# Decoder block on one core: the first loads reordered, in smaller pieces of weights, with one of them issued by ScalarE and nine warming products in place of twelve

## The chip, the cores and the metric

The kernel runs on one core of a Trainium2 chip. The core has TensorE (PE in the profile, with PEld for its weight loads), VectorE (DVE), ScalarE (ACT), GpSimd (POOL) and SyncE (SP), which here only issues transfers. The metric is the time of one execution in device microseconds (us), as the median of a few runs.

## The reference, cut to what matters

One decoder block on 512 tokens of 1024 features: a norm, one wide projection whose parts feed a stick-breaking attention and a recurrence, then a gated merge, an MLP and a gated embedding. The change lies in the first lines only: the norm and the first columns of the projection.

```python
def rms_norm(x, g):
    y = xf * lax.rsqrt(jnp.mean(xf * xf, axis=-1, keepdims=True) + NORM_EPS)
    return y * g
...
h = rms_norm(x, attn_norm_g[i])
u = h @ w_in[i]                       # 1024 x 5376 columns, all of them needed
u_sb, u_rw, u_gate = jnp.split(u, [SB_COLS, SB_COLS + RW_COLS], axis=-1)
q, k, v = jnp.split(u_sb.reshape(bsz, seq, 3 * SB_HEADS, SB_HEAD_DIM), 3, axis=2)
o_sb = stick_breaking_attention(q, k, v)
```

## The kernel before, in words

Activations lie with features on the 128 partitions and tokens along the free axis, so x is eight tiles of 128x512 (`x_in`, one for each k of 0 to 7). The norm is split in two. Each tile of x is multiplied by its gain, a column of the small table `cols`, and goes into the products at once. The factor 1/rms of a token (`rs`) is applied behind the products, when `ps_m` or `ps_z` is read.

Every matrix product is made from three products of rounded parts. A value is split in a high part (ScalarE rounds it: `w_hi`, `h_hi`) and a rest (VectorE subtracts: `w_lo`, `h_lo`). `mm3` issues high by high (L191), rest of x by high weights (L192) and high x by rest of weights (L193). So a tile k of x needs ScalarE (L353) and VectorE (L354) once before any product with it, and each unit of weights needs the same (L221 and L222 in the first two units, L175 and L176 in the later ones).

A unit of weights is 128x1024: eight blocks of 128x128, one for each k. `seq` lists the units in order of use. The first units are q (unit 0), k (unit 1) and v (unit 2) of the first pair of heads, then q, k and v of the second pair (units 3, 4 and 5). For units 0 and 1 the products of both are taken turn by turn for each tile of x, so 6 products for each k, 48 in all. Then come the 24 products of unit 2, then those of unit 3, and so on. The raw weights of a unit go to one of two buffers (`w_raw`), so that the load of unit n waits until the split of unit n-2 is done.

Ahead of the first real product TensorE multiplies a tile of zeros (`warm`) several times.

While the first units are loaded and multiplied, ScalarE squares the tiles of x (L227 for k = 0, L230 for the others, two buffers `sq`), and VectorE sums the squares (`ssum`, L232 and L234). One product (L263) then sums over the partitions; ScalarE and VectorE make `rs` from it (L253 to L257). With `rs`, VectorE reads the first three results (`qT` L394, `kT` L406, `vT` L414), ScalarE and GpSimd round q (`qq`), ScalarE and VectorE split k (`kk`, L409 and L410). TensorE transposes v (L421) and starts the scores (L458).

The instructions are not issued in the order of the code. A scheduler of the framework puts those of each engine into one fixed order when the kernel is built, by its own estimates of when each is ready; a DMA stands in the order of the engine that issues it. At run time each engine takes its instructions in that order and stops at one whose inputs are late. An early difference in the code can so move instructions further on. Each DMA has one of eight semaphores in turn, so an issue waits for the landing of the DMA eight before it.

Of the kernel before, what the change touches and what calls it, by code (L numbers as in the profile page):

```python
# [18 lines left out]
P = 128  # L19
# [66 lines left out]
def tile_block(ctx: ExitStack, tc: tile.TileContext, xT, xt, pT, wts, lora, cols_d, gfin_d, consts_d, out, dbg=None):  # L86
    nc = tc.nc
    act, dve, pool, pe, sync = nc.scalar, nc.vector, nc.gpsimd, nc.tensor, nc.sync
# [3 lines left out]
    def r32(ap):  # L92
        return ap.bitcast(F32)
# [12 lines left out]
    cols = const.tile([P, NCOLS], F32, name="cols")  # L106
# [12 lines left out]
    def col(name, i):  # L119
        return cols[:, COLS[name] + i:COLS[name] + i + 1]  # L120
# [32 lines left out]
    def unit(i):  # L153
        return wts[UBASE[seq[i][0]] + seq[i][1]]
# [65 lines left out]
    def split(hi, lo, src):  # L220
        act.copy(out=hi, in_=src)  # L221
        dve.tensor_tensor(out=lo, in0=src, in1=r32(hi), op=ALU.subtract)  # L222
# [54 lines left out]
    with ExitStack() as sA:  # L277
# [43 lines left out]
        with ExitStack() as s1:  # L321
# [3 lines left out]
            def ps_z():  # L325
                return ps1.tile([P, T], F32, name="ps_z", bufs=5)
# [5 lines left out]
            warm = p1.tile([P, T], BF16, name="warm", tag="sp")  # L332
            pool.memset(warm, 0.0)
            ps = ps_z()
            for _ in range(12):
                pe.matmul(ps, warm[:, 0:P], warm, start=True, stop=True)
            sync.dma_start(out=cols, in_=cols_d)
            ssum = p1.tile([P, T], F32, name="ssum", tag="wl")

            raws = [wpool.tile([P, 1024], F32, name="w_raw", bufs=2) for _ in range(2)]  # L340
            first_w = [[wpool.tile([P, 1024], F32R, name=n) for n in ("w_hi", "w_lo")] for _ in range(2)]
            xs_in = {}

            def first_weights(i, part):
                cs = slice(part * 512, part * 512 + 512)
                sync.dma_start(out=raws[i][:, cs], in_=unit(i)[:, cs])
                split(first_w[i][0][:, cs], first_w[i][1][:, cs], raws[i][:, cs])

            def first_x(k):
                x_in = p1.tile([P, 2, T], F32, name="x_in", tag=("sp", "sph", "spl", "wh")[k // 2]) if k % 2 == 0 else xs_in[k - 1][0]  # L350
                sync.dma_start(out=x_in[:, k % 2, :], in_=xT[:, k, :])
                xs_in[k] = x_in, x_in[:, k % 2, :]
                act.activation(out=h_hi[:, k, :], in_=xs_in[k][1], func=AF.Copy, scale=col("attn_g", k))  # L353
                dve.scalar_tensor_tensor(out=h_lo[:, k, :], in0=xs_in[k][1], scalar=col("attn_g", k), in1=r32(h_hi[:, k, :]),  # L354
                                         op0=ALU.mult, op1=ALU.subtract)


            first_weights(0, 0)
            first_x(0)
            first_weights(1, 0)  # L360
            for k in range(1, 4):
                first_x(k)
            first_weights(0, 1)
            first_weights(1, 1)
            for k in range(4, KT):
                first_x(k)
            loaded.extend(raws)
# [892 lines left out]
    def gated(ps, tt, cs, i, own=False, behind=None):  # L1260

        n = ps.shape[-1]
        t = p4.tile([P, T], F32, name="t4", bufs=3)[:, 0:n]
        s_ = act.activation(out=t, in_=ps, func=AF.Sigmoid, scale=r3[:, tt:tt + 1])
        with tc.issue_after(behind) if behind else nullcontext():
            dve.tensor_tensor(out=t, in0=t, in1=ple[:, tt, cs], op=ALU.mult)
        dve.tensor_tensor(out=xs[:, tt, cs], in0=xs[:, tt, cs], in1=t, op=ALU.add)
        sq = p4.tile([P, T], F32, name="sq4", bufs=2)[:, 0:n]
        sum_ = s4[:, tt, i:i + 1]
        if own:  # L1270
            last = dve.scalar_tensor_tensor(out=sq, in0=xs[:, tt, cs], scalar=1.0, in1=xs[:, tt, cs], op0=ALU.mult, op1=ALU.mult,  # L1271
                                            accum_out=sum_)
        else:
            last = act.activation(out=sq, in_=xs[:, tt, cs], func=AF.Square, accum_out=sum_)
        return s_.ins, last.ins
# [40 lines left out]
    def rest(tt, cs):  # L1316

        ps = ps_main()
        for kk in range(4):
            rows3(ps[:, cs], ws[kk], hx, tt, kk * 2, kk == 0, kk == 3, cs)  # L1320
        return ps[:, cs], tt, slice(512 + cs.start, 512 + cs.stop)
# [3 lines left out]
    for tt in range(TT - 1):  # L1325
        part = rest(tt, slice(0, 512))
        s_, _ = gated(*part, 1)
# [15 lines left out]
    with tc.issue_after(s_):  # L1343
        act.preload_act_table_set(LNEXP)

        r, n = (r4[:, i, tt:tt + 1] for i in (1, 2))
# [3 lines left out]
    with tc.issue_after(sq_):  # L1350
# [4 lines left out]
        cs = COLHALF[1]  # L1355
# [65 lines left out]
```

## Time and profile before

| what | value |
|---|---|
| median of 3 runs | 871.67 us (871.31 to 872.21) |
| profiled execution, its own time | 873.46 us |
| its span in the profile | 871.4 us |
| TensorE busy in the span | 853.4 us, 98% |
| VectorE, ScalarE, GpSimd busy | 678.6, 448.7 and 79.6 us |
| mean granted clock of TensorE | 0.996 |
| DMA queue of the program | 94.46 MB in 32208 packets |

The profiled execution took 873.46 us, 2.06 us more than its span. The prediction's sum is made in the span and carried over to the median as a difference. In the rows of the timeline the first number is the start in us from the span's start, the second the duration. A row that ends in x3 holds three instructions of the same kind in a row, and its duration reaches from the first start to the last end. A bracket at the end tells how long the engine sat idle before the row, and what ended it. L numbers are lines of the kernel before. In the changed kernel the lines from L361 on lie three further down (L424 is what was L421).

### The profile page before, as it was taken

How to read it: one execution, taken by the hardware profiler on the slowest of the kernel's cores; microseconds unless marked ns; L12 is line 12 of the kernel's file. 1: busy time of each engine (PE TensorE's matmuls, PEld its weight loads, DVE VectorE, ACT ScalarE, POOL GpSimd, SP SyncE). 2: the span in 40 equal slices, each digit the busy share in tenths (PEclk: the TensorE clock that was granted, in tenths of full speed). 3: DMA queues.
4: the chain of work that ended last, by engine and by line, in shares of the span. 5: the costliest groups of instructions: out<-in, count | busy, mean ns of one | idle time of the engine just before them, and what ended most of it. 6: DMA issues, size and time to landing. Idle time of an engine off the chain costs nothing.

```text
span 871.4 us, 13421 instructions
## 1 busy us (share of the span) xinstructions
PE 853.4 (98%) x5182; PEld 687.9 (79%) x5182; DVE 678.6 (78%) x1228; ACT 448.7 (51%) x703; POOL 79.6 (9%) x138
## 2 busy tenths in 40 slices
PE   9999999999999999999999999999999999999996
PEld 5778787877777777777888888888888888888885
DVE  7899987896979888666834789858975987697667
ACT  6888887744345343524523555344534543453743
POOL 1432431002202111020000000000000000000000
PEclk9999999999999999999999999999999999999999
DMA  7312212231221224347834720531252035300422
GB/s 268 98 49 68 79 61 84 73 98 50 73 74 61 86 74 158 123 157 262 293 97 150 261 73 24 193 121 49 72 184 107 25 121 168 97 1 0 169 73 97
DMA packets 32272, 95.32 MB, mean 109 GB/s; under 512 B 3664, under 2 KB 3664, under 8 KB 32208
## 3 DMA queue, kind: packets, MB, share of 16 engines
q1 hardware_dynamic: 32208, 94.46, 32.6%
q8 instruction: 41, 0.67, 0.3%
q14 instruction: 23, 0.19, 0.1%
HBM read 83.96 MB, written 10.49 MB: 108 GB/s over the span
## 4 chain that ended last, share of the span: by engine, by line
PE 81%; DVE 10%; ACT 4%; DMA 2%; issue 2%; SPq 0%; POOLq 0%; POOL 0%; ACTq 0%; DVEq 0%
PE ps_m L191 14%; PE ps_m L193 14%; PE ps_m L192 13%; PE ps_m L206 9%; PE ps_m L207 9%; PE ps_m L208 9%; DVE w_lo L176 1%; PE ps_o L497 1%; PE ps_s L941 1%; PE ps_g L903 1%; PE ps_c L932 1%; DVE LX L841 1%; PE ps_g L817 1%; PE ps_z L505 1%; DVE own L828 1%
## 5 line engine op out<-in xcount | busy, mean ns | idle before, releaser
L175 ACT CAST w_hi<-w_raw 128x1024 fp32r<-128x1024 f32 x94 | 99.0, 1053 | 177.2 <-PE ps_m L192 117.2
L176 DVE TENSOR_TENSOR w_lo<-w_raw,w_hi 128x1024 fp32r<-128x1024 f32 x94 | 115.2, 1225 | 37.7 <-ACT w_hi L175 36.9
L191 PE MATMUL ps_m<-h_hi,w_hi 128*128 128x512 f32 x320 | 130.7, 410 | 0.6 <-ACT h_hi L353 0.6
L192 PE MATMUL ps_m<-h_lo,w_hi 128*128 128x512 f32 x320 | 129.0, 403 | 0.0
L193 PE MATMUL ps_m<-h_hi,w_lo 128*128 128x512 f32 x320 | 127.5, 399 | 0.0
L191 PE MATMUL ps_m<-hx,w_hi 128*128 128x512 f32 x256 | 99.6, 390 | 0.4 <-ACT hx L1044 0.4
L192 PE MATMUL ps_m<-hx,w_hi 128*128 128x512 f32 x256 | 99.6, 390 | 0.0
L193 PE MATMUL ps_m<-hx,w_lo 128*128 128x512 f32 x256 | 99.5, 389 | 0.0
L191 PEld LDWEIGHTS ps_m<-h_hi,w_hi 128*128 128x128 f32 x320 | 60.7, 190 | 11.3 <-ACT h_hi L353 1.4
L192 PEld LDWEIGHTS ps_m<-h_lo,w_hi 128*128 128x128 f32 x320 | 60.5, 189 | 11.4 <-DVE h_lo L354 1.2
L193 PEld LDWEIGHTS ps_m<-h_hi,w_lo 128*128 128x128 f32 x320 | 60.3, 188 | 11.7
L191 PEld LDWEIGHTS ps_m<-hx,w_hi 128*128 128x128 f32 x256 | 48.0, 188 | 10.5 <-ACT hx L1044 0.6
L192 PEld LDWEIGHTS ps_m<-hx,w_hi 128*128 128x128 f32 x256 | 48.1, 188 | 10.1 <-DVE hx L1045 0.2
L193 PEld LDWEIGHTS ps_m<-hx,w_lo 128*128 128x128 f32 x256 | 48.1, 188 | 9.9
L206 PE MATMUL ps_m<-w_hi,fS 128*128 128x512 f32 x128 | 49.8, 389 | 0.0
L207 PE MATMUL ps_m<-w_lo,fS 128*128 128x512 f32 x128 | 49.8, 389 | 0.0
L208 PE MATMUL ps_m<-w_hi,fS 128*128 128x512 f32 x128 | 49.8, 389 | 0.0
L1286 POOL TENSOR_SCALAR r<-s 128x1 f32<-128x1 f32 x1 | 0.5, 518 | 480.4 <-DVE sq L1271 480.4
L208 PE MATMUL ps_m<-w_hi,fA 128*128 128x512 f32 x96 | 37.3, 389 | 0.0
L206 PE MATMUL ps_m<-w_hi,fA 128*128 128x512 f32 x96 | 37.3, 389 | 0.0
L207 PE MATMUL ps_m<-w_lo,fA 128*128 128x512 f32 x96 | 37.3, 389 | 0.0
L221 ACT CAST fS<-sums 128x256 fp32r<-128x256 f32 (+1 forms) x32 | 19.9, 620 | 33.3 <-DVE sums L1136 33.3
(378 smaller groups left out, 1913.9 us busy)
## 6 DMA issues: line engine op xcount, KB each, us to landing
w_raw<-in_wts_dram SPq DMA_DIRECT2D x98, 512.0 KB, 3.4
gates<-gg SPq DMA_DIRECT2D x16, 256.0 KB, 2.0
x_in<-in_xT_dram SPq DMA_DIRECT2D x8, 256.0 KB, 5.5
tmp<-gates SPq DMA_DIRECT2D x8, 256.0 KB, 4.2
upsb<-tmp SPq DMA_DIRECT2D x8, 256.0 KB, 3.0
ga<-upsb SPq DMA_DIRECT2D x8, 256.0 KB, 5.7
gb<-gates SPq DMA_DIRECT2D x8, 256.0 KB, 5.3
xs<-in_xt_dram SPq DMA_DIRECT2D x4, 512.0 KB, 7.5
```

Source lines behind the costliest of these rows:

```text
L175: act.copy(out=hi, in_=raw)
L176: dve.tensor_tensor(out=lo, in0=raw, in1=r32(hi), op=ALU.subtract)
L191: pe.matmul(ps, wh, xh[:, k, t], start=first, stop=False)
L192: pe.matmul(ps, wh, xl[:, k, t], start=False, stop=False)
L193: pe.matmul(ps, wl, xh[:, k, t], start=False, stop=last)
L206: pe.matmul(ps, xh[:, k + j], wh, start=first and j == 0, stop=False, skip_group_check=True)
L207: pe.matmul(ps, xh[:, k + j], wl, start=False, stop=False, skip_group_check=True)
L208: pe.matmul(ps, xl[:, k + j], wh, start=False, stop=last and j == 1, skip_group_check=True)
L221: act.copy(out=hi, in_=src)
L497: pe.matmul(ps_o[:, j * P:T], vv[:, j, hh, :, :].rearrange("p a d -> p (a d)"), part[:, ZB[j]:ZB[j] + ZN[j]], start=j == 2 and part is wh, ...
L505: pe.matmul(zt[b][:, :n], tri, part[:, s:s + n], start=False, stop=False, skip_group_check=True)
L817: last = pe.matmul(ps[rows, k], left[rows, k, :], rhs[rows, k], start=True, stop=True)
```

## The change

It does four things in the code of the first loads.

1. The load of `cols` is issued by ScalarE (`act.dma_start`), no longer by SyncE.
2. The first two units of weights are loaded and split in three pieces, of 2, 2 and 4 blocks (128x256, 128x256, 128x512), no longer in two of 4 blocks.
3. The order of the loads is now: unit 0 first quarter, x 0, unit 1 first quarter, x 1, x 2, the second quarters of both, x 3, the halves of both, x 4 to x 7. It was: `cols`, unit 0 first half, x 0, unit 1 first half, x 1, x 2, x 3, the second halves of both, x 4 to x 7.
4. Nine warming products stand where twelve stood.

```diff
-            for _ in range(12):
+            for _ in range(9):
                 pe.matmul(ps, warm[:, 0:P], warm, start=True, stop=True)
-            sync.dma_start(out=cols, in_=cols_d)
+            act.dma_start(out=cols, in_=cols_d)
...
-            def first_weights(i, part):
-                cs = slice(part * 512, part * 512 + 512)
+            def first_weights(i, lo, n):
+                cs = slice(lo * P, (lo + n) * P)
                 sync.dma_start(out=raws[i][:, cs], in_=unit(i)[:, cs])
                 split(first_w[i][0][:, cs], first_w[i][1][:, cs], raws[i][:, cs])
...
-            first_weights(0, 0)
+            first_weights(0, 0, 2)
             first_x(0)
-            first_weights(1, 0)
-            for k in range(1, 4):
-                first_x(k)
-            first_weights(0, 1)
-            first_weights(1, 1)
+            first_weights(1, 0, 2)
+            first_x(1)
+            first_x(2)
+            for i in range(2):
+                first_weights(i, 2, 2)
+            first_x(3)
+            for i in range(2):
+                first_weights(i, 4, 4)
             for k in range(4, KT):
                 first_x(k)
```

The scheduler then orders the engines differently up to about the 210th of TensorE's instructions, and from there as before (apart from line numbers and buffer numbers). Three places matter.

ScalarE, from the start of the program, before:

```order
L124 ACT_TABLE_LOAD
L221 CAST w_hi<-w_raw 128x512
L353 ACTIVATE h_hi<-x_in,cols 128x512
L227 ACTIVATE ssum<-x_in 128x512
L221 CAST w_hi<-w_raw 128x512
L353 ACTIVATE h_hi<-x_in,cols 128x512
L230 ACTIVATE sq<-x_in 128x512
L353 ACTIVATE h_hi<-x_in,cols 128x512 x2
```

ScalarE, the same place, now:

```order
L124 ACT_TABLE_LOAD
L337 DMA cols<-in_cols_dram 128x74
L221 CAST w_hi<-w_raw 128x256
L227 ACTIVATE ssum<-x_in 128x512
L353 ACTIVATE h_hi<-x_in,cols 128x512
L221 CAST w_hi<-w_raw 128x256
L353 ACTIVATE h_hi<-x_in,cols 128x512
L230 ACTIVATE sq<-x_in 128x512
L353 ACTIVATE h_hi<-x_in,cols 128x512
L221 CAST w_hi<-w_raw 128x256 x2
```

The issue of `cols` stands behind the load of the function table, and the first square (L227) now ahead of the first tile's gain (L353). On VectorE the order up to the fifth `h_lo` (k = 4) follows suit: `h_lo` 1, a sum of squares, `h_lo` 2, two quarters of `w_lo`, a sum, `h_lo` 3, two halves of `w_lo`, a sum, `h_lo` 4 to 7.

VectorE where `rs` is made and used, before (the last row of `w_lo` ahead of `qT` is unit 5's):

```order
L536 CAST bones<-first 128x128
L540 CAST caus_b<-first 128x128
L176 TENSOR_TENSOR w_lo<-w_raw,w_hi 128x1024 x2
L256 SCALAR_TENSOR_TENSOR nt<-nt,ps_z 128x512
L257 SCALAR_TENSOR_TENSOR rs<-nt,rs 128x512
L176 TENSOR_TENSOR w_lo<-w_raw,w_hi 128x1024
L394 SCALAR_TENSOR_TENSOR qT<-ps_m,rs 128x512
```

VectorE, the same place, now (the last row of `w_lo` ahead of `qT` is unit 4's; unit 5's follows behind `kk`):

```order
L538 CAST neg<-first 128x128
L539 CAST bones<-first 128x128
L543 CAST caus_b<-first 128x128
L176 TENSOR_TENSOR w_lo<-w_raw,w_hi 128x1024
L256 SCALAR_TENSOR_TENSOR nt<-nt,ps_z 128x512
L257 SCALAR_TENSOR_TENSOR rs<-nt,rs 128x512
L176 TENSOR_TENSOR w_lo<-w_raw,w_hi 128x1024
L397 SCALAR_TENSOR_TENSOR qT<-ps_m,rs 128x512
```

One unit's `w_lo` less stands ahead of `qT`.

TensorE around the transposes of v, in the middle of unit 3's products, before (19 of unit 3's 24 products stand ahead of L421):

```order
L191 MATMUL ps_z<-h_hi,w_hi 128x512
L421 MATMUL ps_m<-cst,vT 128x128 x4
L192 MATMUL ps_z<-h_lo,w_hi 128x512
L193 MATMUL ps_z<-h_hi,w_lo 128x512
L191 MATMUL ps_z<-h_hi,w_hi 128x512
L192 MATMUL ps_z<-h_lo,w_hi 128x512
L193 MATMUL ps_z<-h_hi,w_lo 128x512
L191 MATMUL ps_m<-h_hi,w_hi 128x512
L458 MATMUL ps_z<-qq_271,kk_281 128x256
```

TensorE, the same place, now (12 of unit 3's products stand ahead of L424):

```order
L193 MATMUL ps_z<-h_hi,w_lo 128x512
L424 MATMUL ps_m<-cst,vT 128x128 x4
L191 MATMUL ps_z<-h_hi,w_hi 128x512
L192 MATMUL ps_z<-h_lo,w_hi 128x512
L193 MATMUL ps_z<-h_hi,w_lo 128x512
L461 MATMUL ps_z<-qq_274,kk_284 128x256
```

The transposes stand 7 products earlier in unit 3, and the first scores 10 products earlier. The product of the sums (L263) stands behind 4 of unit 2's products, where it stood behind 7, so counted from the kernel's start the transposes come 7 and the scores 10 products earlier.

## The prediction

> **What bounds the kernel now.** I read the page first, for the share of the engines.
>
> ```profile
> PE 853.4 (98%) x5182; PEld 687.9 (79%) x5182; DVE 678.6 (78%) x1228; ACT 448.7 (51%) x703; POOL 79.6 (9%) x138
> ```
>
> TensorE is busy for 853.4 of 871.4 us. The change removes no real product, so it can only take out time in which TensorE stands still or is held to a slower pace, and only in the part whose order changes, about the first 50 us. The view of waits for 26 to 70 us names two such places in reach (waiter, what it waited for, us in total, times, longest):
>
> ```profile
> PE ps_m L421 <- DVE vT L414: 0.6, 1, 0.6
> PE ps_z L458 <- DVE kk L410: 0.2, 1, 0.2
> ```
>
> The timeline of the first 21 us shows the rest.
>
> ```profile
> 0.73 1.28 ACT L124 ACT_TABLE_LOAD   x1 [0.73 <-PEq L1413]
> 0.74 0.39 SPq L337 DMA_DIRECT2D cols<-in_cols_dram  x1
> 1.18 0.42 SPq L346 DMA_DIRECT2D w_raw<-in_wts_dram  x1
> 1.31 5.30 PE L336 MATMUL ps_z<-warm 128*128 128x512 bf16 x12 [1.31 <-POOL warm L333]
> ...
> 2.59 1.38 SPq L351 DMA_DIRECT2D x_in<-in_xT_dram  x3
> ...
> 4.28 0.62 ACT L221 CAST w_hi<-w_raw 128x512 fp32r<-128x512 f32 x1 [2.27 <-DMA w_raw<-in_wts_dram]
> ...
> 5.28 0.72 ACT L353 ACTIVATE h_hi<-x_in,cols 128x512 fp32r<-128x512 f32 x1 [0.38 <-DMA x_in<-in_xT_dram]
> ...
> 5.91 0.61 ACT L227 ACTIVATE ssum<-x_in 128x512 f32<-128x512 f32 x1
> ...
> 6.06 0.98 PE L191 MATMUL ps_m<-h_hi,w_hi 128*128 128x512 f32 x1
> ...
> 6.85 0.61 PE L192 MATMUL ps_m<-h_lo,w_hi 128*128 128x512 f32 x1
> ...
> 7.29 0.39 PE L193 MATMUL ps_m<-h_hi,w_lo 128*128 128x512 f32 x1
> ...
> 7.96 0.72 ACT L353 ACTIVATE h_hi<-x_in,cols 128x512 fp32r<-128x512 f32 x1 [0.92 <-DMA x_in<-in_xT_dram]
> ...
> 9.98 1.41 DVE L354 SCALAR_TENSOR_TENSOR h_lo<-x_in,cols,h_hi 128x512 fp32r<-128x512 f32 x2
> ...
> 11.31 0.68 DVE L222 TENSOR_TENSOR w_lo<-w_raw,w_hi 128x512 fp32r<-128x512 f32 x1
> ...
> 11.91 0.69 DVE L234 TENSOR_TENSOR ssum<-ssum,sq 128x512 f32<-128x512 f32 x1
> ...
> 13.11 0.75 DVE L354 SCALAR_TENSOR_TENSOR h_lo<-x_in,cols,h_hi 128x512 fp32r<-128x512 f32 x1
> ...
> 13.91 0.50 PE L192 MATMUL ps_m<-h_lo,w_hi 128*128 128x512 f32 x1
> ...
> 16.10 0.39 PE L193 MATMUL ps_m<-h_hi,w_lo 128*128 128x512 f32 x1
> ...
> 18.83 0.39 PE L193 MATMUL ps_m<-h_hi,w_lo 128*128 128x512 f32 x1
> ...
> 19.82 0.69 DVE L234 TENSOR_TENSOR ssum<-ssum,sq 128x512 f32<-128x512 f32 x1
> ...
> 20.64 1.05 PE L263 MATMUL ps_z<-ssum,cst 128*128 128x512 f32 x2
> ```
>
> From 16.10 to 18.83 TensorE issues 12 products, 0.2275 us each, the full pace. The 48 products of units 0 and 1 would fit in 10.9 us, but last from 6.06 to about 19.0. The last stop is the one that counts: at 13.91 TensorE waits for the rest of tile 4, which VectorE ends at 13.11 + 0.75 = 13.86. From there it runs through its remaining 22 products. So the first product's time does not set the end of this stage, and VectorE's queue up to the fifth `h_lo` does. That queue gets dense only when tile 1 has landed, at 7.96, where ScalarE had waited 0.92 for it. The chain is: landing of x 1, ScalarE, a full VectorE, tile 4, TensorE.
>
> **The change part by part.** *Three warming products less.* They lie ahead of the first real product and are in nobody's way. The same timeline cut at 5 us shows nine of them:
>
> ```profile
> 1.31 4.02 PE L336 MATMUL ps_z<-warm 128*128 128x512 bf16 x9 [1.31 <-POOL warm L333]
> ```
>
> Nine end at 5.33, twelve at 6.61, 0.43 each, about half the later pace. If real work starts behind 5.33, the price is nothing; what it can do to the pace is a rival below.
>
> *The issue of `cols` moves.* SyncE's first load goes out 0.44 earlier (0.74 for 1.18), and all behind it too. ScalarE issues `cols` behind its table load, so from 2.01 on. It has nothing else to do until the first weights land. The first user is now the first `h_hi`; its square, which doesn't need `cols`, stands ahead. The view of DMA issues for 0 to 30 us (count, KB each, median us from issue to landing):
>
> ```profile
> x_in<-in_xT_dram SPq DMA_DIRECT2D x8, 256.0 KB, 5.5
> ...
> cols<-in_cols_dram SPq DMA_DIRECT2D x1, 37.0 KB, 1.9
> ```
>
> On an empty queue `cols` took 1.9, a tile of x on a full one 5.5. So it lands between 3.9 and 7.5. I take a time near 4, since ScalarE has a queue of its own with nothing ahead of it, and keep 7.5 for a rival. The Trainium skill ("DMA: Bandwidth & Descriptors", section "Queues, rings and completion order") says that SyncE's and ScalarE's queues have a ring each on the same sixteen DMA engines, which take turns between rings by packets. By that, `cols` would not stand behind SyncE's backlog and the sum would stay as it is; no row of before shows two queues at once.
>
> *The loads in quarters.* Bytes up to and with a tile, in KB (`cols` counted): x 0 had 549 ahead and with it, now 421; x 1 had 1061, now 805; x 2 had 1317, now 1061. The rows give landings of 293 KB at 4.28 (first weights), 549 at 5.28, 1061 at 7.96. Between these, and 0.44 earlier, x 0 lands at 4.28 + 128/256 x 1.00 - 0.44 = 4.34, x 1 at 5.28 + 256/512 x 2.68 - 0.44 = 6.18, x 2 at 7.96 - 0.44 = 7.52. The bounds for x 1 are 5.97 (ScalarE is not free before, next paragraph) and 7.5 (its time from issue, 2.59 to 7.96, unchanged, only issued 0.44 earlier).
>
> ScalarE takes the square at 4.34, `h_hi` 0 at 4.95 to 5.67, a quarter of `w_hi` (about 0.3, half of a half) to 5.97, and `h_hi` 1 at 6.18. The first product comes at about 5.7, 0.36 earlier than now, which by itself is worth nothing. VectorE starts `h_lo` 1 at 6.18 + 0.75. Up to the end of `h_lo` 4 it has three `h_lo` at 0.66 (two in 1.41, the last 0.75 long), three sums and two halves of `w_lo` at 0.60 (11.31 to 11.91), two quarters at 0.30 to 0.60 (I take 0.33, near half of a half), and `h_lo` 4 with 0.75: 1.98 + 1.80 + 1.20 + 0.66 + 0.75 = 6.39. That ends at 13.32, against 13.86. So VectorE's stretch starts earlier, but has grown by the two quarters and by the third sum of squares (0.60), which stood behind `h_lo` 4. The rows of before don't show when x 3 and the second quarters land, only that ScalarE never waited for them; I add 0.25 for one coming late. First term: 13.57 - 13.86 = -0.3, between -0.75 (x 1 at 5.97, nothing late) and +0.8 (x 1 at 7.5).
>
> The sum of squares must keep up, as L263 stands 3 products earlier. Before, VectorE went from `h_lo` 4 at 13.11 to the last sum at 19.82, 6.71 us; one sum less now lies between, so it ends at 12.82 + 6.11 + 0.69 = 19.6. TensorE comes to L263 at 20.64 - 0.3 - 3 x 0.2275 = 19.66: just in time.
>
> *The waits at the transposes and the scores.*
>
> ```profile
> 21.95 3.61 SPq L162 DMA_DIRECT2D w_raw<-in_wts_dram  x2
> 22.90 1.04 ACT L175 CAST w_hi<-w_raw 128x1024 fp32r<-128x1024 f32 x1
> 23.84 0.63 ACT L255 ACTIVATE nt<-rs 128x512 f32<-128x512 f32 x1
> 25.12 0.68 DVE L256 SCALAR_TENSOR_TENSOR nt<-nt,ps_z 128x512 f32<-128x512 f32 x1
> 25.83 0.69 DVE L257 SCALAR_TENSOR_TENSOR rs<-nt,rs 128x512 f32<-128x512 f32 x1
> 26.32 1.05 ACT L175 CAST w_hi<-w_raw 128x1024 fp32r<-128x1024 f32 x1 [1.85 <-DMA w_raw<-in_wts_dram]
> 27.41 1.23 DVE L176 TENSOR_TENSOR w_lo<-w_raw,w_hi 128x1024 fp32r<-128x1024 f32 x1 [0.88 <-ACT w_hi L175]
> 28.55 0.68 DVE L394 SCALAR_TENSOR_TENSOR qT<-ps_m,rs 128x512 f32<-128x512 f32 x1
> 29.27 1.26 ACT L400 CAST qq<-qT 64x512 fp32r<-64x512 f32 x2 [1.89 <-DVE qT L394]
> 30.48 0.66 PE L421 MATMUL ps_m<-cst,vT 128*128 128x128 f32 x4 [0.59 <-DVE vT L414]
> 31.87 1.40 DVE L410 TENSOR_TENSOR kk<-kT,kk 64x512 fp32r<-64x512 f32 x2
> 32.70 0.36 PE L458 MATMUL ps_z<-qq,kk 128*128 128x256 f32 x1 [0.17 <-DVE kk L410]
> ```
>
> Before, `qT` waited behind unit 5's `w_lo`, that for a cast, and that for the load issued at 21.95. Now unit 4's stands there, and the cast of 0.94 ahead of `nt` stands behind it. All of it starts 0.98 earlier with L263, so `nt` ends at 24.47 - 0.98 - 0.94 = 22.55, L256 and L257 (1.40) at 23.95, `w_lo` (1.14) at 25.1, and vT, two reads of 0.60 and one of 0.68 later, at 27.0. TensorE comes to the transposes at 30.48 - 0.59 - 0.3 - 7 x 0.2275 = 28.0. That wait of 0.59 goes. What is late next is `kk`, since ScalarE's cast of unit 5 stands ahead of `qq`. Its load goes out behind unit 3's `w_lo`, 0.9 earlier with the last sum, lands at 25.4, and the cast (1.05), `qq` (1.26), half of `kk` on ScalarE (0.63) and on VectorE (0.70) end at 29.05. TensorE comes there at 32.70 - 0.17 - 0.59 - 0.3 - 10 x 0.2275 = 29.36. So 0.17 goes too, with 0.3 to spare. Second term: -0.76, between -1.5 (some 0.7 of smaller waits between 45 and 50 us go as well) and 0 (the waits come back at the earlier places).
>
> *Sum.* -0.3 - 0.76 = -1.06. The profiled execution, 873.46, would take 872.4; it stands 1.8 above the median, and carried over to that: 871.67 - 1.06 = 870.6. A difference of 0.2%, 1.74 us, is about what a measurement here can tell from none.
>
> **The rivals.** *Tile 1 lands no sooner.* If a load's time on the full queue is fixed (5.4 us from issue), x 1 lands at 7.5, the first term is +0.8, and with the second all is even: 871.7. For it: x 1's 512 KB behind x 0 took 2.68 us, twice as long per byte as those ahead, so something other than the order slows it. Against: there are 256 KB less.
>
> *`cols` lands late* (the slower end). At 7.5, `h_hi` 0 ends at 8.2, `h_hi` 1 starts at 8.5, 2.3 after the forecast, and VectorE's chain ends at 15.7, 1.85 later than now; with the second term 872.8. It decides from a landing behind 6.5 on, where the gain is used up. For it speaks the median of 5.5; against, that only the loads issued before 2.4 can be ahead.
>
> *The pace stays half for longer.* Before, the pace changed between 6.85 (0.61 long) and 7.29 (0.39), some 5.5 to 6 us behind the first warming product. Nine leave TensorE idle from 5.33 to 5.7 and again until 6.18. If it counts anew from 5.7, the pace changes near 11.4; 13 products are done by then, the other 13 ahead of tile 4's rest take 3.0, so to 14.4 for 13.57: 871.4. The Trainium skill ("TensorE: Matmul & The Clock Gate", Part 1) has the clock at half until a free-running window of about 3.4 us was busy; by that the next window would end near 10.5, and the price would be nearer 0.4. The trace agrees on the half pace (0.43 for 0.2275), and no row shows the window.
>
> *All of it comes early.* Tile 1 at 5.97, nothing late, and half of the small waits go too: -0.75 - 0.76 - 0.35, 869.8.
>
> **How the numbers follow.** Forecast 55 in 100, all early 15, tile 1 no sooner 14, the pace 10, `cols` late 6. The predicted time is the forecast's, 870.6. The range takes the early case with half a microsecond of scatter between runs, and the even cases with the same: 869.3 to 872.2. It leaves out most of the late `cols`. Faster by over 0.2% (below 869.93): most of the early case and a little of the forecast, 0.17. Slower by over 0.2% (above 873.41): half of the late `cols` and a rest, 0.05. Within: 0.78.
>
> **What would show it.** Right: `h_hi` 1 at 6.0 to 6.4, `cols` landed ahead of 4.95, the rest of tile 4 done by 13.6, no wait of TensorE at L424 and L461. Wrong: `h_hi` 1 behind 7.5, an idle ScalarE ahead of the first `h_hi` that `cols` ends, products 0.43 apart behind 8 us, or a wait of over 0.5 at L461.

## The result and the profile after

The changed kernel takes 878.36 us (median of 6 runs, 875.84 to 881.10) against 871.94 (871.31 to 872.39) for the kernel before on the same chip: 6.4 us more by the medians. The ratio on record is 1.0066 with a 95% interval of 1.0050 to 1.0082, or 5.8 us. The prediction had 870.6 in 869.3 to 872.2. Two executions of the kernels below, of 1046.07 and 2161.67 us, were slow and are left out of every ratio.

The page of the changed kernel (profiled execution 879.08 us, span 877.2) shows TensorE busy 1.6 us longer, and a new queue, q10, which is ScalarE's. The queue of kind "instruction" is used below.

```profile
PE 855.0 (97%) x5179; PEld 688.3 (78%) x5179; DVE 679.7 (77%) x1230; ACT 449.5 (51%) x705; POOL 78.8 (9%) x138
...
q8 instruction: 41, 0.67, 0.3%
...
q10 hardware_dynamic: 144, 0.04, 0.0%
```

The start, from the timeline of the changed kernel:

```profile
0.74 0.39 SPq L346 DMA_DIRECT2D w_raw<-in_wts_dram  x1
0.76 0.40 ACTq L337 DMA_DIRECT2D cols<-in_cols_dram  x1
...
1.31 3.93 PE L336 MATMUL ps_z<-warm 128*128 128x512 bf16 x9 [1.31 <-POOL warm L333]
...
5.13 0.71 ACT L353 ACTIVATE h_hi<-x_in,cols 128x512 fp32r<-128x512 f32 x1
...
5.89 0.79 PE L191 MATMUL ps_m<-h_hi,w_hi 128*128 128x512 f32 x2 [0.64 <-ACT h_hi L353]
...
7.57 0.72 ACT L353 ACTIVATE h_hi<-x_in,cols 128x512 fp32r<-128x512 f32 x1 [1.44 <-DMA x_in<-in_xT_dram]
...
14.80 0.50 PE L192 MATMUL ps_m<-h_lo,w_hi 128*128 128x512 f32 x1 [0.66 <-DVE h_lo L354]
...
20.84 1.10 PE L263 MATMUL ps_z<-ssum,cst 128*128 128x512 f32 x2
```

In this execution tile 1 came at 7.57, not at 6.18, and TensorE took up the rest of tile 4 at 14.80, for 13.91 before. But the start is the small part. I set products side by side that have the same number of products ahead of them since the first real one (L263 counted, the warming products not), and noted by how much the changed kernel is later. Where this offset grows, time is lost. At 22 us the 60th product stands in both kernels in unit 2, behind L263, first before, then after:

```profile
22.00 0.39 PE L191 MATMUL ps_z<-h_hi,w_hi 128*128 128x512 f32 x1
```

```profile
22.93 0.40 PE L191 MATMUL ps_z<-h_hi,w_hi 128*128 128x512 f32 x1
```

| place in the program | offset at it, us |
|---|---|
| unit 2, at 22 us | +0.93 |
| behind the first scores, from 50 us | +0.83 |
| up to 140 us | +0.84 |
| from 156 us | +2.42 |
| from 284 us | +2.78 |
| from 306 us | +5.86 |
| end | +5.90 |

The start carries 0.9 us of it, with the late tile 1, and nothing is added up to 140 us. Then come two large steps of 1.58 and 3.08 us, at 145 and 304 us, far behind everything that the change touches. The view of TensorE's waits for 40 to 320 us names them (waiter, what ended the wait, us in total, times, longest):

```profile
PE ps_g L820 <- issue: 1.9, 2, 1.7
...
PE ps_g L622 <- ACT lx L614: 1.0, 1, 1.0
```

The first is a stop in which TensorE waited for nothing that the trace shows. It sits in the middle of a burst of 64 small products, in the timeline after:

```profile
299.96 0.75 PE L820 MATMUL ps_g<-LX,own 32*32 32x32 f32 x64
...
301.72 0.85 PE L820 MATMUL ps_g<-LX,LB 32*32 32x64 f32 x42
304.31 0.53 PE L820 MATMUL ps_g<-LX,LB 32*32 32x64 f32 x22 [1.73 <-issue]
```

Before, the same burst ran through:

```profile
298.94 1.10 PE L817 MATMUL ps_g<-LX,LB 32*32 32x64 f32 x64
```

The table of stretches (busy us and count of PE, PEld, DVE, ACT, POOL, then the granted clock) shows that the clock falls behind the stop (it is 0.50 from 306 to 308 us), which is the other half of the 3.08:

```profile
302.00:305.00 3.00, 1.27 (x61) 1.01 (x50) 0.79 (x2) 0.98 (x2) 0.00 (x0) 1.00 0.03 8
305.00:309.00 4.00, 4.00 (x72) 2.63 (x71) 3.02 (x7) 1.67 (x2) 0.00 (x0) 0.57 0.19 70
```

The second large step begins with a copy on VectorE, 2.38 us for 0.20. First after, then before:

```profile
145.19 2.38 DVE L842 COPY X<-cst 128x64 f32<-128x64 f32 x1 [3.15 <-DMA o_sb<-oo]
145.20 0.53 POOL L584 MEMSET keep<- 128x512 f32 x1 [15.42 <-DMA o_sb<-oo]
...
146.55 0.96 POOL L599 MEMSET Z<- 128x1024 f32 x1
...
151.35 0.50 PE L622 MATMUL ps_g<-lx,lw 128*128 128x512 f32 x1 [0.96 <-ACT lx L614]
```

```profile
144.28 0.20 DVE L839 COPY X<-cst 128x64 f32<-128x64 f32 x1 [3.08 <-DMA o_sb<-oo]
...
144.47 0.53 POOL L581 MEMSET keep<- 128x512 f32 x1 [15.53 <-DVE X L839]
```

Both copies wait for the same transfer, the last load of `o_sb`, and so does GpSimd's first memset for the recurrence. Before, GpSimd started 0.19 behind VectorE, when the copy was done. After, it started 0.01 behind, and the copy ended only when GpSimd's nine memsets had (146.55 + 0.96 = 147.51; 145.19 + 2.38 = 147.57).

### The profile page after: what moved, and what is told of

It reads as the page before. It is cut to its first block, busy times and chain, and to the rows that moved or that the text cites. A ratio compares the mean times of both kernels' runs of the same rounds, so it can differ in the third digit from the quotient of the medians.

```text
span 877.2 us, 13421 instructions
## 1 busy us (share of the span) xinstructions
PE 855.0 (97%) x5179; PEld 688.3 (78%) x5179; DVE 679.7 (77%) x1230; ACT 449.5 (51%) x705; POOL 78.8 (9%) x138
## 4 chain that ended last, share of the span: by engine, by line
PE 83%; DVE 10%; ACT 4%; issue 2%; DMA 1%; SPq 0%; POOL 0%; POOLq 0%; DVEq 0%; ACTq 0%
PE ps_m L191 14%; PE ps_m L193 13%; PE ps_m L192 13%; PE ps_m L206 9%; PE ps_m L208 9%; PE ps_m L207 9%; DVE w_lo L176 1%; PE ps_g L820 1%; PE ps_z L508 1%; PE ps_o L500 1%; PE ps_s L944 1%; PE ps_c L935 1%; PE ps_g L906 1%; DVE LX L844 1%; PE ps_g L191 1%
```

## The experiments

All ratios are to the kernel before in the same rounds, with the 95% interval.

**Which of the four parts costs.** Theories: the order and timing of the start (1), the length of TensorE's instruction stream, which nine warming products make three products shorter (2), and ScalarE's queue (3).

Nine warming products alone (kernel before, `range(12)` to `range(9)`):

> The kernel before with one edit: nine warming products instead of twelve. Every engine's other instructions stand in the order of before. Theory 2 (the three products taken away shift TensorE's instruction stream against the blocks in which it is fetched, and the shifted stream stops in the dense bursts at 253, 304 and 361 us): 4 to 6 us slower than before, about 877, with a TensorE stop of over 1 us that waits for nothing, near 304 us, and a clock below 0.7 in the slices behind it. Theory 1 (the new order and timing of the first 40 us) and theory 3 (ScalarE's DMA queue): within 0.5 us of before, 871.4 to 872.4, no stop at 304.

873.91 us, 1.0034 (1.0019 to 1.0048). Twelve in the changed kernel (`range(9)` to `range(12)`):

> The changed kernel with one edit: twelve warming products again. All else stands in the changed kernel's order. Theory 2 (fetch blocks of TensorE's stream): the stop at 304 us goes and with it 4 to 5 us, so about 873.5, 0.2 to 0.3% over before; the 2.4 us VectorE copy at 145 us stays. Theory 1 and theory 3: no change from the changed kernel, 876 to 880.

873.41 us, 1.0027 (1.0015 to 1.0040). `cols` by SyncE in the changed kernel (`act.dma_start` to `sync.dma_start`):

> The changed kernel with one edit: the norm's columns loaded by SyncE's queue again, so that ScalarE issues no DMA. Theory 3 (the second queue costs transfers or instruction fetch later): 3 to 6 us less than the changed kernel, 872 to 875, with no TensorE stop at 304. Theory 1 and theory 2: 876 to 880 as the changed kernel; at the start h_hi of the first tile waits for the columns until about 5.5 to 6 us.

876.36 us, 1.0060 (1.0048 to 1.0072). `cols` by ScalarE alone (kernel before, `sync.dma_start` to `act.dma_start`):

> The kernel before with one edit: the norm's columns loaded by ScalarE's queue. The scheduler puts some of TensorE's first 220 instructions in another order for it. Theory 3: 3 to 6 us slower than before, 875 to 878, with a stop of TensorE in a dense burst at 250 to 360 us. Theory 2: within 1 us of before. Theory 1: the start moves by some tenths of a us and the copy at 145 us may collide, so 871 to 874.

870.53 us, 0.9990 (0.9981 to 0.9999). Theory 3 falls: the queue costs nothing, and alone it is the only part that gains, by 0.2% at most. Theory 2 holds for the stop (the price for nine alone was guessed too high, and the clock did not fall in its trace): the kernels with nine stop for 1.6 to 2.1 us near 300 us, those with twelve don't. The copy of 2.38 us is in all three kernels with the quarters and in none without. So the loss has two separate causes.

**Why three products fewer stop TensorE 300 us later.** The 41 packets of queue q8, 0.67 MB, are 16 KB each. I located them in time by narrowing the window of the DMA view to 0.13 us. This is where they show, in windows of 4 us: the kernel before from 292 to 296 (and none to 300), the kernel with nine alone none from 292 to 296, and one from 296 to 300.

```profile
q8 instruction: 1, 0.02, 2.3%
```

```profile
q8 instruction: 1, 0.02, 1.4%
```

The packet moves 3.5 us, though that execution stood 1.1 us ahead of before. Between lies the first burst of the group, whose first product waits for VectorE's `own`, in the kernel with nine alone:

```profile
295.48 0.43 DVE L848 TENSOR_TENSOR own<-X,cst 128x256 f32<-128x256 f32 x1
...
296.14 0.75 PE L817 MATMUL ps_g<-LX,own 32*32 32x32 f32 x64
...
300.39 0.53 PE L817 MATMUL ps_g<-LX,LB 32*32 32x64 f32 x22 [1.63 <-issue]
```

Theory: the next block is asked for when TensorE's sequencer, which runs ahead of the array, passes a fixed place in the stream. With twelve that place lies just ahead of the waiting product, with nine behind it. To restore the length without the time, three short products replace the three long ones:

```diff
-            for _ in range(12):
-                pe.matmul(ps, warm[:, 0:P], warm, start=True, stop=True)
+            for n in [T] * 9 + [8] * 3:
+                pe.matmul(ps[:, 0:n], warm[:, 0:P], warm[:, 0:n], start=True, stop=True)
```

> The kernel before with nine long warming products and three short ones behind them (8 columns each), so that TensorE's instruction stream is as long as with twelve. All else stands in the order of before. Theory of the fetch (a block of TensorE's instructions is asked for when its sequencer passes a fixed place in the stream; three products fewer put that place behind the first instruction of the burst near 296 us, which waits for VectorE): no stop at 300 us, the fetch packet near 294 us again, and the 1.0 us that the nine gained by 50 us is kept: 869.9 to 870.9, 0.0 to 1.2 less than before. Rival (fewer long warming products, a colder TensorE, or the earlier start itself bring the stop): the stop of 1.6 us at 300 us stays, 873 to 874.

870.92 us, 1.0005 (0.9995 to 1.0014), no stop, packet at 295.0, 2.7 ahead of the burst. The same with two and with one short product:

> The kernel before with nine long and two short warming products: TensorE's stream is one product shorter than with twelve, and the fixed place at which block 16 of its instructions is asked for moves one product on. Theory of the fetch: the place is either still ahead of the burst's first product or behind it. So the fetch packet comes near 294 us and there is no stop, with 870.9, or it comes 2 us behind the burst's start, with a stop of 1.5 to 1.8 us and 872.5 to 873.9; nothing between, and once the stop is there it is there with fewer products too. Rival (each missing product costs a third of the stop): 0.5 us of stop, 871.5.

> The kernel before with nine long and one short warming product, so that the stream is two products shorter than with twelve. Theory of the fetch: none of the stop or all of it (1.5 to 1.8 us), and all of it if the kernel with two short ones has it. Rival (a third for each missing product): 1.1 us of stop, 872.

874.62 us, 1.0037 (1.0023 to 1.0052), stop 1.73; and 874.00 us, 1.0033 (1.0021 to 1.0045), stop 1.84. One missing product is enough, and there is no third of a stop. Over the traces used here:

| length of the stream | kernels | packet against the burst's first product | stop at 300 us |
|---|---|---|---|
| as with twelve | 9 | 2.6 to 2.9 us ahead | none |
| 1, 2 or 3 products short | 6 | 1.8 to 2.2 us behind | 1.6 to 2.1 us, ends 4.2 to 4.6 behind |

With 1, 2 and 3 products missing in the kernel before, the stop comes behind 40, 41 and 42 of the burst's 64: the edge of the block moves with the stream. In four of the six short ones the stop and the slower products behind it cost 3.1 to 3.3 us in all, since the clock falls (0.57 above); in two only 1.6.

Whether the clock falls goes with how long TensorE stood still. The kernel before has such a case too, far from the change:

```profile
405.36 0.63 PE L984 MATMUL ps_c<-cst,y 128*128 128x128 f32 x4 [1.97 <-DVE y L979]
```

From 29 us to the last products, the fifteen traces have six stops of 1.84 to 2.18 us, whatever TensorE waited for, and all six are followed by about 3.4 us at a clock of 0.5. Of five stops of 1.72 to 1.82 us one is (the 1.73 above), and of seven of 1.37 to 1.65 none. So a stop near this edge costs 1.2 to 1.6 us more in one execution than in another. Over all executions the mean granted clock is 0.9947 to 0.9964 in the seven short kernels and 0.9960 to 0.9976 in the nine others; by the span, a difference of 0.002 is an estimated 1.7 us. The case at L984 is in the traces of the kernel before and of the changed kernel (a wait of 2.18 there), so it is not part of the offset at the end.

That the request goes out when the sequencer passes a place is inferred from these times; no row shows the request itself. Streams of full length stop too where another edge falls in a burst (0.55 us at 355.74 before, 1.23 at 358.15 with three short products in the changed kernel), and the 0.36 that the changed kernel lost between 156 and 284 us holds such a stop of 0.18. The Trainium skill ("Runtime: NRT & Kernel Launch", section "Instruction fetch mechanics") describes instructions refilled in blocks of 16 KiB, 256 each, by the sequencer's own queue, and calls the cost mostly hidden. The size agrees with 41 packets of 0.67 MB; hidden it is not here, with stops up to 2.08 us.

**Why the copy collides.** The change has two loads more (quarters). All loads take the eight DMA semaphores in turn, so the last `o_sb` signals number 7, where it signalled 5. GpSimd's memset waits for seven of the eight one after the other; number 5 was third in its list, number 7 is last. Two dummy loads in the kernel before do the same to it:

```diff
                 if hh == 1:
                     sync.dma_start(out=o_sb[:, hp, :], in_=oo)
+                    for j in range(2 if hp == 0 else 0):
+                        sync.dma_start(out=turn[:, j:j + 1], in_=cols_d[:, j:j + 1])
```

> The kernel before with two added loads of 512 bytes to a tile that nobody reads, near 30 us; all engines' other instructions stand as in before. They turn the ring of eight DMA semaphores by two, so that the last load of o_sb ahead of 145 us signals number 7, as in the changed kernel, for 5. GpSimd waits for seven of the eight, one after the other, and number 7 stands last in its list (5 is third). Theory of the semaphores: GpSimd's first memset starts together with VectorE's copy of X near 144.5 us, the copy takes 2.3 us for 0.20, TensorE waits some 1 us for lx at L614, and the kernel takes 1.2 to 2.2 us more than before: 872.2 to 873.2. Rival (the quarters' new order sets the collision): the copy takes 0.20, 870.8 to 871.3.

872.35 us, 1.0017 (1.0008 to 1.0026). Its trace:

```profile
144.49 2.38 DVE L842 COPY X<-cst 128x64 f32<-128x64 f32 x1 [3.17 <-DMA o_sb<-oo]
144.50 0.53 POOL L584 MEMSET keep<- 128x512 f32 x1 [15.43 <-DMA o_sb<-oo]
```

The order of all engines is that of before, so the collision needs nothing but the number of loads. In the changed kernel, the loads can be as many as before if the second and third piece of a unit come together; three short products keep the length of the stream in this version too:

```diff
+                ls = slice(lo * P, (lo + (6 if lo == 2 else n)) * P)
+                if lo < 4:
+                    sync.dma_start(out=raws[i][:, ls], in_=unit(i)[:, ls])
```

> The changed kernel with nine long and three short warming products, and with the second and third piece of each of the first two units loaded together (768 columns) and split in two as in the change. That makes as many loads as before, so o_sb signals number 5 again, without an added load; in this kernel's list for GpSimd it stands fifth of seven. The scheduler reorders some early rows. Semaphores: GpSimd starts 0.05 to 0.15 behind VectorE's copy; if that is late enough, a copy of 0.2, and 870.0 to 871.5; if not, a copy of 2.3 and 871.7 to 873. If the quarters themselves cost the start 1 us beside all this: 871.5 to 872.5 with a short copy.

871.48 us, 1.0002 (0.9990 to 1.0014). Number 5 stands fifth there:

```profile
144.50 0.20 DVE L844 COPY X<-cst 128x64 f32<-128x64 f32 x1 [3.08 <-DMA o_sb<-oo]
144.61 0.56 POOL L586 MEMSET keep<- 128x512 f32 x1 [15.44 <-DMA o_sb<-oo]
```

So GpSimd's delay behind VectorE goes with the place in the list: 0.24 us in second place (the two kernels with four added loads), 0.19 in third, 0.11 in fifth, 0.01 to 0.02 in last, and only the last brings the long copy. The Trainium skill ("SBUF — State Buffer", section "Who interferes with whom") says that a VectorE copy in a two-port mode and GpSimd exclude each other, and that the first to issue keeps the ports for its whole instruction. The trace agrees that one waits for the other, but not on the length: the copy had to wait for nine memsets, 2.31 us, not for one of 0.53. By the recorded starts the copy was the first by 0.01 us and lost, so who issued first at the ports is not to be read from these rows, and none shows the copy's mode.

**Both together, and what is left for the start.** Three short products alone in the changed kernel, as in the diff above; four dummy loads alone (`range(4 ...)`, `o_sb` signals number 3, second in the list); both; and nine warming products with `cols` by ScalarE, without the quarters:

> The changed kernel with one repair alone: nine long and three short warming products. No load is added, and every engine keeps the changed kernel's order. If the wait for kk (0.8 and 1.8 us) in the two kernels with four added loads is the price of those loads, it is 0.2 to 0.3 here. Fetch and semaphores: no stop at 300 us, a copy of 2.4 us at 145 us, 1.0 to 2.0 over before: 872.0 to 873.0, as with twelve long ones. If the short products cost the start its pace: 873.5 to 874.

872.59 us, 1.0011 (0.9997 to 1.0024).

> The changed kernel with one repair alone: four added loads of 512 bytes near 30 us turn the ring of semaphores so that GpSimd's wait for o_sb stands second in its list. Nine warming products as in the change. Both theories: a copy of 0.20 at 145 us, and still the stop of 1.5 to 2 us at 300 us with its slower products behind it: 1.3 to 2.0 us less than the changed kernel, 3.5 to 5 over before, so 874.5 to 876.

873.05 us, 1.0024 (1.0006 to 1.0041): less than expected. Its profile has the short copy and a stop of 1.85.

> The changed kernel with both repairs: nine long and three short warming products, and four added loads of 512 bytes near 30 us that turn the ring of semaphores so that GpSimd's wait for o_sb stands second in its list of seven. All else stands in the changed kernel's order. If the fetch and the collision are the two causes: no stop at 304 us, a copy of 0.20 at 145 us, and 871.0 to 872.0, since the start itself was 0.2 to 0.8 us behind at 50 us. If the quarters or the second queue cost something else later: 873.5 to 878.

872.09 us, 1.0014 (1.0003 to 1.0024): a little above what was expected, with a short copy and no stop at 300 us. In the two kernels with four dummy loads TensorE waits 1.8 and 0.8 for `kk`, against 0.2 to 0.4 in the others with the changed kernel's order. So the dummy loads have a price of their own, and the repair without them, `a_s3_q6` above, comes out even with before.

> The kernel before with the norm's columns by ScalarE's queue and nine warming products, without the quarters. Both theories: no collision at 145 us (as many loads as before, so the same semaphores), the stop of 1.5 to 2 us at 300 us with its price of about 3: 2 to 3.5 over the same kernel with twelve, 872.5 to 874.

873.25 us, 1.0025 (1.0008 to 1.0041): the stop's price again, without any quarters (its trace is not used).

The version that the theories point to, halves, `cols` by ScalarE, and nine long with three short products:

> The kernel before with two parts of the change: the norm's columns by ScalarE's queue, and nine long with three short warming products. The loads stay in halves and in the order of before, the number of loads too, so the semaphores stand as before. If the theories hold, neither the stop nor the collision: 869.3 to 870.5, 0.5 to 1.7 under before, and under every other kernel. If the first product only waits longer for x 1, it is as with the twelve: 870.5.

870.50 us, 0.9993 (0.9983 to 1.0004). With twelve long ones (`b_act`, 870.53) the interval ends at 0.9999. Both beat the changed kernel by some 0.7%; against before, 0.1% is the most that is there.

## Why the prediction was wrong

**The step that failed** is the premise that the change acts "only in the part whose order changes, about the first 50 us", with the three warming products at a price of "nothing". So no term of the sum stood for what lies behind 50 us. The order of the engines is equal from there on, and I took equal order for equal time. Two things that no order shows had changed, the place of block edges in TensorE's stream and the number of the semaphore of each load. By experiment they cost:

| cause | measured by | price |
|---|---|---|
| stream three products shorter | nine alone less nine and three short, 1.0034 and 1.0005 | 2.5 us |
| the same, in the changed kernel | changed kernel less twelve or three short, 1.0066 and 1.0027 or 1.0011 | 3.4 or 4.8 us |
| two loads more | two dummy loads in the kernel before, 1.0017 | 1.5 us |
| all the rest of the change | pieces of 2 and 6 with short products, 1.0002 | 0.2 us, not told from nothing |

The interval of each ratio is 0.8 to 1.5 us to either side, so the prices are rough. The last three rows make 5.1 or 6.5 us; the whole is 5.8 by the ratio. The terms do not simply add: the changed kernel without the collision (1.0024, 1.0006 to 1.0041) is 3.7 us under it, more than twice the collision's own price. An estimate of 1.3 us of this goes with the clock, 0.9962 for 0.9947 on the mean of all executions. What else the two stalls do to each other was not settled.

**Warming products at no cost.** Right for the start of this execution and wrong for the kernel. Nine end at 5.24 (1.31 + 3.93), ahead of the first product, and the pace was full from about 7 us on. But the rival of the half pace is real: in four of the eleven traces with nine long warming products (`b_warm9s3`, `b_warm9s2`, `b_act_s3`, `a_s3_q6`) products stand 0.43 apart behind 8 us, and in none of the four with twelve. In `a_s3_q6`:

```profile
8.17 0.63 PE L193 MATMUL ps_m<-h_hi,w_lo 128*128 128x512 f32 x1
8.60 0.63 PE L191 MATMUL ps_m<-h_hi,w_hi 128*128 128x512 f32 x1
```

The cover that I named held here; the price of this run came from their number in the stream.

**`cols` near 4.** Right. It was issued at 0.76, beside the table load and not behind it, and took 2.9 us; no `h_hi` waited for it.

**x 1 at 6.18, first term -0.3.** In the profiled execution of the changed kernel the rival took place, at its price: 7.57, with the rest of tile 4 done at 14.75 (14.00 + 0.75; before 13.86) and +0.93 at 22 us, for +0.8. My reason for that rival was misread: by the rows, 512 KB in 2.68 us is 1.3 times as long per byte as the 256 KB in 1.00, not twice. But the landing scatters between executions. In the five other traces with the quarters `h_hi` 1 started at 6.17 to 6.75, in the eight with halves at 7.3 to 8.6. The one with three short products alone runs through the prediction's own numbers:

```profile
6.32 0.72 ACT L353 ACTIVATE h_hi<-x_in,cols 128x512 fp32r<-128x512 f32 x1 [0.80 <-DMA x_in<-in_xT_dram]
...
18.44 0.39 PE L193 MATMUL ps_m<-h_hi,w_lo 128*128 128x512 f32 x1
...
19.72 1.12 PE L263 MATMUL ps_z<-ssum,cst 128*128 128x512 f32 x2
```

`h_lo` 4 ends there at 13.50 (12.75 + 0.75; predicted 13.57), the last of the 48 products starts 0.39 ahead of before (18.44 for 18.83), and L263 comes at 19.72 (19.66). One execution on each side is not enough, though. On the mean `h_hi` 1 starts at 6.54 in the six traces with quarters and at 7.83 in the eight with halves, 1.3 us earlier, for the 1.8 of the prediction (6.18 for 7.96). VectorE's stretch from there to the end of `h_lo` 4 is 7.3 us for 5.9, as predicted (7.4). So the rest of tile 4 is done at 13.81 with quarters and at 13.73 with halves: the term was too large by its landing, and is not told from nothing.

**Second term -0.76.** It came out at its bound, near 0. From 22 to 50 us the offset changes by -0.10 to +0.11 in the four traces with the changed order (the changed kernel, `a_warm12`, `a_s3`, `a_sync`). The wait at the transposes went, as predicted, and TensorE was at them at 27.97 in the kernel with short products (28.0). But waits came back at later places that I had not followed, in the changed kernel:

```profile
PE ps_z L508 <- DVE spl L222: 0.3, 1, 0.3
PE ps_z L512 <- DVE spl L222: 0.3, 1, 0.3
PE ps_z L461 <- DVE kk L413: 0.2, 1, 0.2
```

With 0.31 for `wl` at L500 they make 1.06, against 0.92 before. The bound of 0, "the waits come back at the earlier places", was the right idea: what went at the transposes came back, only later in the program.

**The sum.** Start and scores together come to about -0.1 to +0.2 in the kernels with twelve or with short products (offsets at 50 us of +0.20 and -0.07), for -1.06. By itself that would have been no change that can be measured, and `a_s3_q6` at 1.0002 is that: inside the range, but without the gain that the sum gave. The 6 us came from outside the sum. A chance of 0.05 for slower was too low for a change that alters the count of instructions and of loads ahead of 800 us of other work.

## What to carry to other kernels

An edit at the start can change two counts that everything behind depends on: how many instructions stand in an engine's stream and how many loads have been issued. If the same instructions in the same order take longer far from the edit, look for a stop that waits for nothing (then for the instruction packet ahead of it), and for two engines released by one transfer whose starts have moved by tenths of a us. Before reading an edit's worth from such a kernel, make a version with the counts restored, by short instructions or by pieces joined. And compare several executions where a load ends the wait: here one landing moved by 1.4 us, and a stop of nearly the same length brought a fall of the clock in one trace and none in another.

## What the runs showed of the hardware

- The queue of kind "instruction" moves 41 packets of 16 KB, one for about 253 of TensorE's 10358 products and weight loads. In a dense stretch (64 products in 0.75 to 1.1 us) TensorE can run out of them: from the burst behind which the packet comes to the end of the stop there are 4.2 to 4.6 us, of which its products fill about 2.6. That the packets are TensorE's is inferred from their number and their times.
- A single product of 8 columns at the start decided on 2.8 us of the whole, by a stop near 300 us (1.0037 with two, 1.0005 with three).
- All six stops of TensorE of 1.84 to 2.18 us were followed by a clock of 0.5 for about 3.4 us, one of five of 1.72 to 1.82 us was, and none of seven of 1.37 to 1.65 us.
- GpSimd's waits on several semaphores take about 0.045 us each (0.24 - 0.01 over five places), and 0.1 us decided whether a copy of 0.20 us took 2.38.
- ScalarE issued a transfer at 0.76 us, while its table load ran from 0.73 to 2.01.
